# A transformer block's input projection turned from direct products into Strassen's seven block products over two halves of the tokens

## The chip, the cores and the metric

The kernel runs on one core of a Trainium2 chip. The metric is the device time of one execution in microseconds (us); the time of the kernel before is a median over three runs. One more execution was recorded by the hardware profiler, and all rows below are from that one. Matrix products run on TensorE (PE in the rows; PEld is its weight load), element-wise work on VectorE (DVE), ScalarE (ACT) and GpSimd (POOL), and transfers are issued by SyncE (SP) and POOL, in the order of each engine's queue.

## The reference

One block on x of 2048 tokens × 1024 features: RMSNorm, an input projection to 3080 columns, two attentions side by side, an output projection and a SwiGLU FFN. What the change touches is the norm and the projection; the rest consumes its parts.

```python
h = rmsnorm(x, norm1_g[l])
proj = jnp.einsum('bsd,de->bse', h, w_in[l])
dq, dk, dv, fq, fk, fv, fg = jnp.split(proj, SPLITS, axis=-1)
dq = rope_partial(dq.reshape(B, S, DIFF_HEADS, 2, DIFF_DH), cos, sin)
dk = rope_partial(dk.reshape(B, S, DIFF_HEADS, 2, DIFF_DH), cos, sin)
...
log_f = jax.nn.log_sigmoid((fg + b_f[l]).astype(f32))
cum = jnp.cumsum(log_f, axis=1).transpose(0, 2, 1)
```

The parts dq, dk, dv, fq, fk, fv are 512 columns each, fg (the gates) 8. `cum` is a bias of the second attention.

## The kernel before

Every product is made of fp32r operands in pairs: a value is split into a high part (a cast, on ACT) and a low part (the difference, on DVE), and one product becomes three matmuls, high × high, low × high and high × low, that add up in the same PSUM bank (`mm3`, L255 to L257). A matmul has a contraction of 128 and up to 512 columns.

The projection is the first stage (`c1`, L145 to L449). Tokens are in four chunks of 512 (c), each of four rows of 128 (t); features are in eight blocks of the contraction (k). Per chunk, x is loaded (`load_x`), normed (`norm`, `norm_two`: squares on ACT or DVE, the reciprocal root on POOL, a scaling), transposed by PE and evicted straight into the pair `hTh[c]`, `hTl[c]` (`turn`, `turn_two`), which stay in SBUF for the whole stage. Then come, in program order:

- e = 0 to 3 of `w_e` (fq), chunk by chunk, with the norm and the transposes of the next chunk between them;
- e = 4 to 7 (fk); then fv and the gates per row t, from `t_major` with 256 and 264 columns (the last 8 are the gates);
- the gates' log-sigmoid, 16 small transposes and a running sum along tokens (`forget_sums`);
- e = 8 and 9, which hold the rotary features of dq and dk together, with the rope on DVE and POOL;
- e = 10 to 15 (the rest of dq and dk), and dv per row.

`e_major` is 24 matmuls of 512 columns: weights of one e (128 columns of output, which land on the partitions), one chunk of tokens. Each result is split again into a pair (`split_psum`, L141 and L142) and stored to DRAM by POOL, from where the attention stage loads it.

The FFN of the same kernel (`c4`), which the change does not touch, already uses seven block products: a unit there is 7 products of 12 matmuls, in `ORDER` P1, P2, P6, P5, P7, P3, P4, with three PSUM banks (A, B, C) that are added to and taken in between. Its lines L1061 to L1063 are the three matmuls, L1071 and L1073 copies and sums of a bank into `u`, L818 and L819 the splits; L1179 to L1181 are the matmuls of the down projection. Queues of engines are in the order that a list scheduler gives them from program order, data and buffers.

## Time and profile before

| | us |
|---|---|
| median of 3 runs | 2855.63 (2855.2 to 2855.87) |
| the profiled execution | 2852.41 |
| its span | 2850.6 |
| TensorE busy | 2786.9 (98%) |
| VectorE busy | 1706.1 (60%) |
| ScalarE busy | 1359.1 (48%) |
| first product of the projection starts | 10.30 |
| first attention score starts | 571.51 |

The span is the profiled execution from its first to its last instruction on the core, and the execution's own time is 1.8 us longer. The busy time of TensorE is modelled from pipelined matmuls, so 98% does not say that it works at its peak; the distance between starts of matmuls says how fast it goes.

### The profile page before, as it was taken

To read this page: it belongs to the slowest core of one execution; us is meant where nothing else is said; L and a number is where in the kernel's file an instruction comes from. 1 tells how busy PE (TensorE), PEld (TensorE's weight loads), DVE (VectorE), ACT (ScalarE), POOL (GpSimd) and SP (SyncE) were. 2 spreads that over 40 slices of the span, in tenths; PEclk is the share of its full clock that TensorE was granted. 3 is DMA by queue.
4 is the path that set the end of the run, shared out by engine and by line. 5 is a ranking of instruction groups with operands and counts; after the bars stand their busy time and mean duration, and the time that the engine had idled before them with its cause. 6 is when DMAs were issued, how large, how long until landed. Compare 5 with 4: busy or idle time off the path is not lost.

```text
span 2850.6 us, 40932 instructions
## 1 busy us (share of the span) xinstructions
PE 2786.9 (98%) x14538; PEld 2331.8 (82%) x14538; DVE 1706.1 (60%) x3509; ACT 1359.1 (48%) x2764; POOL 613.0 (22%) x1087
## 2 busy tenths in 40 slices
PE   8999999999999999998999999999999999999998
PEld 7889888889989987787877777877888788888887
DVE  5321411088898898887253766665776666665555
ACT  5221211177888787887344333333554433333444
POOL 3210542033434333332111111111000111110001
PEclk9999999999999999999999999999999999999999
DMA  5342444345424332433465544435766333334665
GB/s 195 129 144 90 130 131 126 129 123 145 113 71 123 83 98 77 110 86 118 181 202 196 185 162 160 156 130 194 244 235 223 119 101 103 111 110 133 228 198 173
DMA packets 160860, 410.94 MB, mean 144 GB/s; under 512 B 24544, under 2 KB 41072, under 8 KB 160656
## 3 DMA queue, kind: packets, MB, share of 16 engines
q1 hardware_dynamic: 117488, 282.87, 32.1%
q0 software_dynamic: 43136, 125.45, 12.5%
q8 instruction: 114, 1.87, 0.3%
q14 instruction: 90, 0.74, 0.1%
q10 hardware_dynamic: 32, 0.01, 0.0%
HBM read 274.44 MB, written 133.76 MB: 143 GB/s over the span
## 4 chain that ended last, share of the span: by engine, by line
PE 75%; issue 13%; POOL 4%; ACT 3%; DMA 2%; DVE 2%; POOLq 0%; SPq 0%; DVEq 0%; ACTq 0%
PE psM L257 6%; PE psM L256 6%; PE psM L255 6%; PE ps L709 6%; PE psF L1061 6%; PE psF L1062 5%; PE psF L1063 5%; PE psF L1180 4%; PE psF L1181 4%; PE psF L1179 4%; PE psS L552 4%; PE psS L553 4%; PE psO L644 3%; PE psO L638 2%; PE psO L637 2%
## 5 line engine op out<-in xcount | busy, mean ns | idle before, releaser
L1061 PE MATMUL psF<-hhP,wop 128*128 128x512 f32 x1232 | 478.4, 394 | 16.7 <-DVE u L1073 11.7
L1062 PE MATMUL psF<-hlP,wop 128*128 128x512 f32 x1232 | 480.9, 390 | 0.0
L1063 PE MATMUL psF<-hhP,wop 128*128 128x512 f32 x1232 | 479.9, 390 | 0.0
L582 ACT ACTIVATE p_sb<-p_sb,mx 128x1024 f32<-128x1024 f32 (+7 forms) x384 | 343.7, 901 | 25.0 <-DVE mx L563 17.6
L1061 PEld LDWEIGHTS psF<-hhP,wop 128*128 128x128 f32 x1232 | 231.6, 188 | 83.1 <-DVE u L1073 22.9
L552 PE MATMUL psS<-ks,q 128*128 128x512 f32 (+2 forms) x640 | 271.4, 424 | 3.8 <-DVE mx L569 3.4
L1063 PEld LDWEIGHTS psF<-hhP,wop 128*128 128x128 f32 x1232 | 231.7, 188 | 49.1 <-DVE wop L819 0.2
L1062 PEld LDWEIGHTS psF<-hlP,wop 128*128 128x128 f32 x1232 | 231.8, 188 | 44.8
L709 PE MATMUL ps<-ident,p_sb 128*128 128x128 f32 x1632 | 250.6, 274 | 9.2 <-ACT thd L735 5.3
L1180 PE MATMUL psF<-dop 128*128 128x512 f32 x616 | 239.8, 389 | 0.0
L1181 PE MATMUL psF<-dop 128*128 128x512 f32 x616 | 239.7, 389 | 0.0
L1179 PE MATMUL psF<-dop 128*128 128x512 f32 x616 | 239.7, 389 | 0.0
L553 PE MATMUL psS<-ks,q 128*128 128x512 f32 (+2 forms) x640 | 232.9, 365 | 0.0
L709 PEld LDWEIGHTS ps<-ident,p_sb 128*128 128x128 f32 x1632 | 194.2, 141 | 40.4 <-ACT thd L735 7.5
L255 PE MATMUL psM<-hTh,whi 128*128 128x512 f32 (+1 forms) x528 | 206.1, 392 | 0.4 <-ACT hTh L222 0.3
L256 PE MATMUL psM<-hTl,whi 128*128 128x512 f32 (+1 forms) x528 | 205.6, 390 | 0.6 <-DVE hTl L223 0.5
L257 PE MATMUL psM<-hTh,wlo 128*128 128x512 f32 (+1 forms) x528 | 205.3, 389 | 0.0
L818 ACT CAST wop<-sP 128x512 fp32r<-128x512 f32 x176 | 109.1, 622 | 196.0 <-PE psF L1063 188.3
L818 ACT CAST dop<-wr 128x512 fp32r<-128x512 f32 x154 | 95.5, 620 | 200.0 <-PE psF L1181 185.2
L819 DVE TENSOR_TENSOR dop<-wr,dop 128x512 fp32r<-128x512 f32 x154 | 106.2, 690 | 133.6 <-ACT dop L818 133.4
L1071 ACT COPY u<-psF 128x512 f32<-128x512 f32 x132 | 77.6, 588 | 196.5 <-PE psF L1063 196.5
L819 DVE TENSOR_TENSOR wop<-sP,wop 128x512 fp32r<-128x512 f32 x176 | 120.9, 688 | 81.1 <-ACT wop L818 80.7
(215 smaller groups left out, 6067.4 us busy)
## 6 DMA issues: line engine op xcount, KB each, us to landing
ar<-a_d SPq DMA_DIRECT2D x70, 512.0 KB, 3.5
wr<-in_w_gate_dram SPq DMA_DIRECT2D x44, 512.0 KB, 4.7
wr<-in_w_up_dram SPq DMA_DIRECT2D x44, 512.0 KB, 4.9
a_d<-u POOLq DMA_DIRECT2D x88, 256.0 KB, 3.5
wr<-wd_d SPq DMA_DIRECT2D x40, 512.0 KB, 4.0
a_d<-t POOLq DMA_DIRECT2D x66, 256.0 KB, 2.9
q<-fq_d SPq DMA_DIRECT2D x64, 256.0 KB, 4.1
q<-dq_d SPq DMA_DIRECT2D x64, 256.0 KB, 3.8
```

What stands on the lines that cost most here:

```text
L255: nc.tensor.matmul(ps, lh, rh, start=k == 0, stop=False)
L256: nc.tensor.matmul(ps, lh, rl, start=False, stop=False)
L257: nc.tensor.matmul(ps, ll, rh, start=False, stop=k == DK - 1)
L552: nc.tensor.matmul(pm[:, 0:mw], q[:, m, 0, qc], ks[:, m, cols], start=True, stop=False)
L553: nc.tensor.matmul(pm[:, 0:mw], q[:, m, 1, qc], ks[:, m, cols], start=False, stop=not last)
L709: nc.tensor.transpose(ps[:, (2 * i + s) * P:(2 * i + s + 1) * P], p_of(u, s, m, k0 + i), ident)
L1061: nc.tensor.matmul(acc, o[:, 0, ks_], hh[:, k, :], start=first and k == 0, stop=False, **go)
L1062: nc.tensor.matmul(acc, o[:, 0, ks_], hl[:, k, :], start=False, stop=False, **go)
L1063: nc.tensor.matmul(acc, o[:, 1, ks_], hh[:, k, :], start=False, stop=k == 3, **go)
L1179: nc.tensor.matmul(acc, a[:, 0, bs], w[:, 0, :], start=first and m == 0, stop=False, **go)
L1180: nc.tensor.matmul(acc, a[:, 0, bs], w[:, 1, :], start=False, stop=False, **go)
L1181: nc.tensor.matmul(acc, a[:, 1, bs], w[:, 0, :], start=False, stop=m == NF // 2 - 1, **go)
```

## The change

The projection's stage is written anew. Tokens are in two halves of two chunks, features of the contraction in two halves of four blocks (`kh`), weights in pairs of e; one unit, `Features(half, e)`, makes e and e + 1 for both chunks of a half by seven products of 12 matmuls in place of 96 in `e_major`. `Values(half)` does the same for fv and dv together, with 4 × 12 matmuls for each of the seven products. h is kept only as the seven combined operand pairs (`ops_p`, tiles `phP1`, `plP1` and so on), for one half at a time.

Chunks 0 and 1 with e = 0 to 3 are still made by `e_major`, now from the operands P1, P2 (chunk 0) and P4, P3 (chunk 1). Transposed blocks go to a tile `hb` first (`turn`), from there to DRAM (`hop_d`) and into a split. `quarter` loads blocks of both chunks from `hop_d` as `hr`, makes four differences on DVE, and splits them into P5, P7 and P6, or stores them to DRAM (`tp_d`): P4 of the first half, all four of the second. `load_op` and `put_op` bring them back.

Then 14 units and two halves of values follow: six units of the first half, the values of both halves, eight units of the second half. From the fourth step on, the norm, transposes and quarters of the second half and the sums of value weights (`value_sums`, to `wv_d` in DRAM) run as a generator beside the six first units. The second half's operands take the place of the first half's while the first half's values are made. The gates are 32 matmuls per half with 16 or 8 rows of output and 512 tokens along the columns, so their sum runs along the free side and needs no transposes. The rope's subtract and add move from POOL to DVE.

```diff
+        hop, opp, rawp, hx = pool("hopP", 1), pool("opP", 6), pool("rawP", 4), pool("hx", 6)
...
-        def turn(c, rows, k):
-            ps = psT.tile([P, 512], F32, name="psT")
-            for t4 in range(4):
...
+        def turn(c, q, kh, rows, p=None):
+            b = hxt([P, 4, 256], "hb")
...
                         nc.tensor.transpose(ps[:, (2 * ki + i) * P:(2 * ki + i + 1) * P],
-                                            rows[i][:, (k0 + ki) * P:(k0 + ki + 1) * P], ident)
+                                            rows[i][:, k * P:(k + 1) * P], ident)
...
-                    nc.scalar.activation(hTh[c][:, k, hs], pv, AF.Copy, scale=gcol[:, 0, k:k + 1])
-                    nc.vector.scalar_tensor_tensor(
-                        hTl[c][:, k, hs], pv, gcol[:, 0, k:k + 1], f32(hTh[c][:, k, hs]), ALU.mult, ALU.subtract)
+                    if ki:
+                        nc.vector.tensor_scalar(b[:, k0 + ki, :], pv, gcol[:, 0, k:k + 1], None, ALU.mult)
+                    else:
+                        nc.scalar.activation(b[:, k0 + ki, :], pv, AF.Copy, scale=gcol[:, 0, k:k + 1])
+            nc.gpsimd.dma_start(out=hop_d[c, kh, q], in_=b)
+            if p:
+                cs = slice(q * 256, (q + 1) * 256)
+                split(ops_p[p][0][:, :, cs], ops_p[p][1][:, :, cs], b)
...
+        def quarter(half, q, k0, early):
+            cs, ks_ = slice(q * 256, (q + 1) * 256), slice(k0, k0 + 2)
+            def put(p, src):
+                if early and p != "P4":
+                    hi, lo = ops_p[p]
+                    split(hi[:, ks_, cs], lo[:, ks_, cs], src)
+                else:
+                    nc.gpsimd.dma_start(out=tp_d[p][half, k0 // 2, q], in_=src)
+            b = {}
...
+                    nc.sync.dma_start(out=r[:, kh], in_=hop_d[half * 2 + c, kh, q][:, ks_])
+                    b[kh, c] = r[:, kh]
+            b11, b21, b12, b22 = b[0, 0], b[1, 0], b[0, 1], b[1, 1]
+            yield
+            nc.vector.tensor_sub(b11, b12, b11)
+            nc.vector.tensor_sub(b12, b22, b12)
+            put("P5", b11)
+            put("P7", b12)
+            yield
+            nc.vector.tensor_sub(b22, b22, b11)
+            nc.vector.tensor_sub(b21, b21, b22)
+            put("P6", b22)
+            put("P4", b21)
+            yield
...
+        def load_op(half, p):
+            r = [hxt([P, 4, 256], "hr") for _ in range(2)]
+            for q in range(2):
+                if p in tp_d:
+                    for k in range(2):
+                        nc.sync.dma_start(out=r[q][:, 2 * k:2 * k + 2], in_=tp_d[p][half, k, q])
+                else:
+                    c, kh = dict(P1=(0, 0), P2=(0, 1), P3=(1, 1))[p]
+                    nc.sync.dma_start(out=r[q], in_=hop_d[2 * half + c, kh, q])
+            return p, r
...
+            def multiply(self, p):
+                o, (hh, hl) = self.op.pop(p), ops_p[p]
+                first = p in FIRST_OF
+                if first:
+                    self.bank[FIRST_OF[p]] = bank()
+                acc = self.bank[BANK_OF[p]]
+                for k in range(4):
+                    ks_ = slice(k * P, (k + 1) * P)
+                    go = dict(skip_group_check=not first)
+                    nc.tensor.matmul(acc, o[:, 0, ks_], hh[:, k, :], start=first and k == 0, stop=False, **go)
+                    nc.tensor.matmul(acc, o[:, 0, ks_], hl[:, k, :], start=False, stop=False, **go)
+                    nc.tensor.matmul(acc, o[:, 1, ks_], hh[:, k, :], start=False, stop=k == 3, **go)
...
+            def take(self, p):
+                acc, d = self.bank[BANK_OF[p]], self.dst
+                if p in ("P1", "P6", "P7"):
+                    i = dict(P1=(0, 0), P6=(0, 1), P7=(1, 1))[p]
+                    d[i] = ut()
+                    nc.scalar.copy(d[i], acc)
+                    if p == "P7":
+                        nc.vector.tensor_add(d[1, 1], self.bank["B"], d[1, 1])
+                        self.done(1, 1)
+                elif p == "P2":
+                    nc.vector.tensor_add(d[0, 0], acc, d[0, 0])
+                    self.done(0, 0)
...
+            def multiply(self, p, k):
+                o, (hh, hl) = self.op.pop((p, k)), ops_p[p]
+                first, last = p in FIRST_OF, k == 3
+                if first and k == 0:
+                    self.bank[FIRST_OF[p]] = [bank() for _ in range(4)]
+                for b in range(4):
+                    acc, bs = self.bank[BANK_OF[p]][b], slice(b * P, (b + 1) * P)
+                    go = dict(skip_group_check=not first)
+                    nc.tensor.matmul(acc, hh[:, k, bs], o[:, 0, :], start=first and k == 0, stop=False, **go)
+                    nc.tensor.matmul(acc, hh[:, k, bs], o[:, 1, :], start=False, stop=False, **go)
+                    nc.tensor.matmul(acc, hl[:, k, bs], o[:, 0, :], start=False, stop=last, **go)
...
+        def value_sums(k):
+            r = [raw("wv") for _ in range(2)]
+            for kh in range(2):
+                rows = slice((kh * 4 + k) * P, (kh * 4 + k + 1) * P)
+                for i in range(2):
+                    nc.sync.dma_start(out=r[kh][:, i], in_=w_t[rows, i * 520:i * 520 + 512])
+            yield
+            a11, a12, a21, a22 = r[0][:, 0], r[1][:, 0], r[0][:, 1], r[1][:, 1]
+            o = hlt([P, 2, 512], F32, "vs")
+            nc.vector.tensor_add(o[:, 0], a21, a22)
+            nc.vector.tensor_sub(o[:, 1], o[:, 0], a11)
...
-        turn_two(0, 0, rows[0:2])
+        we = {0: split_e(r0)}
+        for kh in range(2):
+            turn(0, 0, kh, rows[0:2], ("P1", "P2")[kh])
...
-        for c in range(NCH):
-            nxt = [load_x(4 * c + 4 + i) for i in range(4)] if c + 1 < NCH else None
-            for e in range(4):
-                if c == 0 and e < 2:
-                    ps = e_major(we[e], 0, pq[e], halves_[1])
-                else:
-                    ps = e_major(we[e], c)
-                if nxt and e < 2:
...
+        for e in range(4):
+            if e < 2:
+                ps = e_major(we[e], 0, pq[e], halves_[1])
+            else:
+                ps = e_major(we[e], 0)
+            if e < 2:
+                we[e + 2] = split_e((r2, r3)[e])
+                norm_two(nxt[2 * e:2 * e + 2])
+            else:
+                for kh in range(2):
+                    turn(1, e - 2, kh, nxt[2 * (e - 2):2 * (e - 1)], ("P4", "P3")[kh])
+                we[e - 2] = split_e(raw_e(e - 2))
+            give(e, 0, ps)
+        rest = [raw_e(2), raw_e(3)]
+        first = [Features(0, e) for e in (4, 6, 10, 12, 14, 8)]
+        last = [Features(1, e) for e in range(0, 16, 2)]
+        vals = [Values(0), Values(1)]
+        steps = [("in", u, p) for u in first for p in ORDER]
+        n_first = len(steps)
+        for v in vals:
+            steps += [("val", v, p, k) for p in ORDER for k in range(4)]
...
+        for e in range(4):
+            ps = e_major(we[e], 1)
+            if e < 2:
+                we[e + 2] = split_e(rest[e])
+            quarters = quarter(0, e % 2, e // 2 * 2, True)
+            for _ in quarters:
+                pass
+            give(e, 1, ps)
+            if e == 2:
+                advance_loads(0)
+                advance_sums(6)
...
+            z = hxt([P, 2, 512], "gz")
+            for j in range(2):
+                todo_ = [((0, "P1"), (4, "P2")), ((8, "P3"), (12, "P7"))][j]
+                ps = bank()
+                for m, (w0, p) in enumerate(todo_):
+                    hh, hl = ops_p[p]
+                    for k in range(4):
+                        w = gop[:, w0 + k]
+                        st, sp_ = m + k == 0, m == 1 and k == 3
+                        both = w.rearrange("p a b -> p (a b)")
+                        if not sp_:
+                            nc.tensor.matmul(ps[0:16, :], both, hh[:, k, :], start=st, stop=False)
+                        nc.tensor.matmul(ps[0:8, :], w[:, 0, :], hl[:, k, :], start=False, stop=False)
+                        if sp_:
+                            nc.tensor.matmul(ps[0:16, :], both, hh[:, k, :], start=False, stop=True)
+                g, g2 = ut("g"), ut("g2")
+                nc.scalar.copy(g[0:16, :], ps[0:16, :])
+                nc.sync.dma_start(out=g2[0:8, :], in_=g[8:16, :])
...
+            nxt = load(0)
+            yield
+            ahead = []
+            for n, (c, q) in enumerate(todo_):
+                rows, nxt = nxt, None
+                for r in rows:
+                    norm(r)
+                    yield
+                for kh in range(2):
+                    turn(c, q, kh, rows)
+                    yield
+                if n + 1 < len(todo_):
+                    nxt = load(n + 1)
+                for a in ahead:
+                    yield from a
+                ahead = []
+                if c == 3:
+                    ahead = [quarter(1, q, k0, False) for k0 in (0, 2)]
+            for a in ahead:
+                yield from a
+            for k in range(4):
+                yield from value_sums(k)
...
+        for at, s in enumerate(steps):
+            val = s[0] == "val"
+            advance_loads(at)
+            advance_sums(at + 7)
+            advance_splits(at + (3 if val else 4))
+            s[1].multiply(*s[2:])
+            if not val:
+                s[1].take(s[2])
+                if at < n_first:
+                    if at == 0:
+                        waiting.append(load_op(0, "P4"))
+                    elif at == 2:
+                        put_op(*waiting.pop(0))
+                    elif at > 2:
+                        next(bg, None)
+                    if at == n_first - 1:
+                        for _ in bg:
+                            pass
+                        gates(0)
             else:
-                wt = load_t(520, 512)
-            for c in range(NCH):
...
-            nc.scalar.copy(o.rearrange("p h d -> p (h d)"), ps)
-            nc.gpsimd.dma_start(out=dv_d[t * P:(t + 1) * P], in_=o)
```

Three places of the queues, in the kernel's own names. First ScalarE at the very start, before (`xt` is x, `s2` the sums of squares, `whi` the first weights' high part, `hTh0` chunk 0):

```order
L191 ACT_TABLE_LOAD
L191 ACTIVATE psM_153,s2_152<-xt_132 128x512
L191 ACTIVATE psM_163,s2_162<-xt_134 128x512
L199 ACTIVATE xt_132<-xt_132,rstd_151 128x512
L199 ACTIVATE xt_134<-xt_134,rstd_161 128x512
L235 CAST whi_174<-wraw_136 128x1024
L222 ACTIVATE hTh0_121<-psT_178,gcol_80 128x256
L222 ACTIVATE hTh0_121<-psT_187,gcol_80 128x256
```

ScalarE at the same place now (`we` are the first weights, `wop` their pair):

```order
L159 ACT_TABLE_LOAD
L159 CAST wop_195<-we_157 128x512
L222 ACTIVATE psF_174,s2_173<-xt_153 128x512
L222 ACTIVATE psF_184,s2_183<-xt_155 128x512
L229 ACTIVATE xt_153<-xt_153,rstd_172 128x512
L229 ACTIVATE xt_155<-xt_155,rstd_182 128x512
L159 CAST wop_198<-we_157 128x512
L222 ACTIVATE psF_240,s2_239<-xt_159 128x512
L248 ACTIVATE hb_201<-psF_202,gcol_80 128x256
L248 ACTIVATE hb_201<-psF_209,gcol_80 128x256
L248 ACTIVATE hb_219<-psF_220,gcol_80 128x256
```

The cast of half of the first weights moved ahead of the squares, and the transposed blocks go to `hb` first.

Second, VectorE before, behind the last two chunks' norm and around the end of the fourth chunk's query products:

```order
L181 TENSOR_SCALAR xt<-xt,rstd 128x1024
L142 TENSOR_TENSOR hl<-psM,hl 128x512 x2
L207 SCALAR_TENSOR_TENSOR hTl_128<-psT,gcol,hTh_127 128x512 x4
L142 TENSOR_TENSOR hl<-psM,hl 128x512
L207 SCALAR_TENSOR_TENSOR hTl_128<-psT,gcol,hTh_127 128x512 x2
L236 TENSOR_TENSOR wlo<-wraw,whi 128x1024
L207 SCALAR_TENSOR_TENSOR hTl_128<-psT,gcol,hTh_127 128x512 x2
L142 TENSOR_TENSOR hl<-psM,hl 128x512 x4
L338 TENSOR_SCALAR sublnb<-sublnb 128x128
```

VectorE now, at the end of chunk 1's query products (`hr` are loaded blocks, `plP5` to `plP7` low parts of operands, `wop_873` the low part of the first unit's first weights):

```order
L160 TENSOR_TENSOR hl_781<-psF_739,hl_781 128x512
L160 TENSOR_TENSOR plP6_141<-hr_767,phP6_140 128x2x256
L274 TENSOR_TENSOR hr_830<-hr_830 128x512
L160 TENSOR_TENSOR plP5_143<-hr_827,phP5_142 128x2x256
L278 TENSOR_TENSOR hr_830<-hr_830,hr_827 128x512
L160 TENSOR_TENSOR plP7_145<-hr_830,phP7_144 128x2x256
L279 TENSOR_TENSOR hr_827<-hr_827,hr_830 128x512
L160 TENSOR_TENSOR plP6_141<-hr_830,phP6_140 128x2x256
L160 TENSOR_TENSOR hl_844<-psF_802,hl_844 128x512
L637 TENSOR_SCALAR sublnb_81<-sublnb_81 128x128
L646 TENSOR_TENSOR lp_858<-lamv_853 128x128
L160 TENSOR_TENSOR wop_873<-we_786,wop_873 128x512
```

Eviction splits, which stood with norms and transposes, now stand between differences and splits of the quarters, and behind these the first unit's weights.

Third, TensorE before, where a block of transposes of the next chunk stands in the query products:

```order
L257 MATMUL psM<-hTh_121,wlo 128x512
L205 MATMUL psT<-ident,xt 128x128 x8
L255 MATMUL psM<-hTh_121,whi 128x512
L256 MATMUL psM<-hTl_122,whi 128x512
L257 MATMUL psM<-hTh_121,wlo 128x512
```

TensorE now, in the first unit between its products P7 (`phP_144`) and P3 (`phP_146`); `phP_949` is P4:

```order
L431 MATMUL psF<-phP_144,wop 128x512
L240 MATMUL psF<-ident,xt 128x128 x6
L429 MATMUL psF<-phP_949,wop 128x512
L430 MATMUL psF<-plP_950,wop 128x512
L431 MATMUL psF<-phP_949,wop 128x512
L429 MATMUL psF<-phP_949,wop 128x512
L430 MATMUL psF<-plP_950,wop 128x512
L429 MATMUL psF<-phP_146,wop 128x512
```

Transposes that stood between two e now stand inside a unit, and a part of P4 was moved ahead of P3.

## Rows read from the trace of the kernel before

**Rows 1.** The profiled page: busy time by engine, TensorE's granted clock by slices.
```profile
PE 2786.9 (98%) x14538; PEld 2331.8 (82%) x14538; DVE 1706.1 (60%) x3509; ACT 1359.1 (48%) x2764; POOL 613.0 (22%) x1087
...
PEclk9999999999999999999999999999999999999999
```

**Rows 2.** Groups of TensorE, 0 to 572 us: count, busy us, mean ns, idle.
```profile
L255 PE MATMUL psM<-hTh,whi 128*128 128x512 f32 x496 | 196.5, 396 | 0.0
...
L255 PE MATMUL psM<-wt,hTh 128*128 128x512 f32 x128 | 50.5, 394 | 0.0
...
L255 PE MATMUL psM<-wt,hTh 128*128 128x264 f32 x128 | 36.6, 286 | 0.0
```

**Rows 3.** Windows: length, then busy us (count) of each engine, clock, DMA share, GB/s.
```profile
122.00:571.00 449.00, 448.26 (x2318) 381.30 (x2317) 91.50 (x157) 72.58 (x129) 116.85 (x197) 1.00 0.39 124
1557.00:1992.00 435.00, 422.60 (x1841) 342.04 (x1842) 285.99 (x444) 163.09 (x279) 65.53 (x121) 1.00 0.50 167
```

**Rows 4.** Timeline of ScalarE, 71 to 73 us: start, us, instruction, idle before.
```profile
72.19 0.59 ACT L141 CAST hl<-psM 128x512 fp32r<-128x512 f32 x1 [3.23 <-PE psM L257]
```

**Rows 5.** Timeline of ScalarE, 118 to 135 us.
```profile
127.40 0.59 ACT L141 CAST hl<-psM 128x512 fp32r<-128x512 f32 x1 [4.01 <-PE psM L257]
132.95 0.59 ACT L141 CAST hl<-psM 128x512 fp32r<-128x512 f32 x1 [4.96 <-PE psM L257]
```

**Rows 6.** Timeline of TensorE around the first attention score.
```profile
571.51 0.28 PE L552 MATMUL psS<-ks,q 128*128 128x256 f32 x1
```

**Rows 7.** Timeline of all engines from the start.
```profile
4.39 0.60 ACT L191 ACTIVATE psM<-xt 128x512 f32<-128x512 f32 x1 [1.46 <-DMA xt<-in_x_dram]
...
6.85 0.72 ACT L199 ACTIVATE xt<-xt,rstd 128x512 f32<-128x512 f32 x1 [0.42 <-POOL rstd L138]
...
8.68 1.03 ACT L235 CAST whi<-wraw 128x1024 fp32r<-128x1024 f32 x1
...
9.74 1.23 DVE L236 TENSOR_TENSOR wlo<-wraw,whi 128x1024 fp32r<-128x1024 f32 x1 [1.21 <-ACT whi L235]
...
10.30 0.58 PE L255 MATMUL psM<-hTh,whi 128*128 128x256 f32 x1
```

**Rows 8.** Timeline of VectorE in the first FFN half.
```profile
1577.20 0.68 DVE L819 TENSOR_TENSOR wop<-wr,wop 128x512 fp32r<-128x512 f32 x1
1577.80 0.68 DVE L1014 TENSOR_TENSOR sP<-sP,wr 128x512 f32<-128x512 f32 x1
```

**Rows 9.** Timeline of ScalarE in the second FFN half: one unit apart.
```profile
2242.28 0.59 ACT L1071 COPY u<-psF 128x512 f32<-128x512 f32 x1 [2.04 <-PE psF L1063]
...
2261.43 0.59 ACT L1071 COPY u<-psF 128x512 f32<-128x512 f32 x1 [2.04 <-PE psF L1063]
```

**Rows 10.** Timeline of TensorE in the down projection, 69 products apart.
```profile
2029.97 0.39 PE L1179 MATMUL psF<-dop 128*128 128x512 f32 x1
...
2045.61 0.39 PE L1179 MATMUL psF<-dop 128*128 128x512 f32 x1
```

**Rows 11.** Timeline of TensorE: a block of transposes and the next product.
```profile
71.99 1.04 PE L205 MATMUL psT<-ident,xt 128*128 128x128 f32 x8
72.78 0.48 PE L255 MATMUL psM<-hTh,whi 128*128 128x512 f32 x1
```

**Rows 12.** Waits of TensorE, 1540 to 1992 us: total us, times, longest.
```profile
PE psF L1061 <- DVE u L1073: 10.5, 9, 1.9
PE psF L1061 <- DVE hlP L819: 2.5, 1, 2.5
```

**Rows 13.** Timeline of TensorE: attention's first product with values.
```profile
586.00 0.36 PE L637 MATMUL psO<-th,v 128*128 128x256 f32 x1
```

**Rows 14.** DMA issues: queue, count, KB each, median us to landing.
```profile
xt<-in_x_dram SPq DMA_DIRECT2D x16, 512.0 KB, 5.7
...
v<-fv_d SPq DMA_DIRECT2D x8, 1024.0 KB, 5.4
...
h_d<-h2b POOLq DMA_DIRECT2D x14, 512.0 KB, 4.6
```

454 lines of the change are left out of this document (271 added, 183 removed).

## The prediction

> **What bounds the kernel now.** I read the page first: busy times of the engines and the granted clock [rows 1]. TensorE is busy for 2786.9 of 2850.6 us and its clock stands at 9 tenths or more in every slice, so the program ends when TensorE has gone through its queue; VectorE (60%) and ScalarE (48%) matter only where TensorE stands and waits for them. Next the groups of TensorE up to 572 us, shapes apart [rows 2]: three lines of 496 products 512 columns wide, three of 128 such with `wt`, and six groups of 128 that are 256 or 264 wide. Then the windows [rows 3]: from 122 to 571 us TensorE is busy for 448.26 of 449.00 us, so this stretch has no gap to win; it gets shorter by fewer or quicker products alone.
>
> Three places date the stage. The eviction behind the eighth query product (chunk 1, e = 3) starts at 72.19 [rows 4]; two evictions in the middle stand 5.55 us apart for 24 products, 0.2313 us each [rows 5]; the first attention score, right behind the last product, starts at 571.51 [rows 6]. From 72.2 to 571.5 the old program therefore needs 499.3 us. The profiled execution took 2852.41 us, the median of the runs is 2855.63, so I work on the profiled time and add 3.2 at the end.
>
> **What the change does to the queue of TensorE.** In columns over 512: before 1488 + 384 products, 768 of about half that width (390 together) and 96 halves (48) make 2310. After: 8 × 24 classical ones for the first four feature groups, 14 units × 84 (seven block products of 12), values 2 × 336, gates 2 × 32: 2104. So 206 go.
>
> **Up to the first unit.** The order shows the classical products of chunks 0 and 1 with e = 0 to 3 unchanged in number, but their start is later. Before, the first square on ScalarE runs at 4.39, the scaling at 6.85, the weight cast at 8.68, its low half on VectorE from 9.74, and the first product at 10.30 [rows 7]. Now a cast of the first weights stands ahead of the squares; its weights are the third transfer of SP's queue, which was issued 0.9 us behind x. I take 2.5 us for that. Each transposed block now goes through one more step (eviction to `hb`, a 1.03 us cast, a 1.23 us subtract in place of the direct one): 3.2 us more. First product about 16.0, 5.7 later. Before, 61.9 us lay between first product and eighth eviction for 44.4 us of full products and 6 of transposes, so about 11 were lost there; a later start should win back about 4 of them. The eighth product then ends at 73.9. VectorE has about 62 operations up to the last split of chunk 1, then 37 rows of quarters, splits and sums ahead of the low half of the first unit's weights; with one operation of 512 elements every 0.60 us [rows 8] these are about 60 us from 4.4 on, so they end at about 64 if they never wait, at 74 with 10 us of waiting. I take **F = 74** for the first unit, between 68 (all 11 us won back but one) and 82 (the quarters, which go to DRAM and return, end 8 us later).
>
> **From F on.** A unit of the later FFN has the same form: 84 products in 19.15 us, 0.228 each [rows 9]. 14 units: 268.2. Values have the form of the down projection, 69 products from 2029.97 to 2045.61, 0.2267 each [rows 10]: 672 of them are 152.3. The 64 gate products have 16 or 8 rows of output but still 512 columns, at the same price 14.5. The later half's 64 transposes stay on the queue: 8 take 0.79 us [rows 11], so 6.3. Together 441.3.
>
> **Which rate.** The 0.2313 of the old products and the 0.2267 to 0.228 of the FFN are different forms in the same trace; the new products are written as the FFN's, but the stage is the old one's, with other transfers. If they ran at 0.2313, 1912 products would cost 7.7 more. I take half, +4, bounds 0 and 8. The Trainium skill, "TensorE: Matmul & The Clock Gate", section "Wait — 56ns, not 53.3ns?", says that warm matmuls start N ÷ 2.4 GHz plus about 2.5 ns apart, 215.7 ns at 512 columns, for any form. This trace does not agree in size: [rows 5] have 231.3 and [rows 10] 226.7. By that rule only the 206 products count, 44.4 us instead of 58 less 4, an estimate which would put the result near 2830; the measured rows decide.
>
> **Stalls.** The first half of the FFN's feature stage, with the background work beside it, takes 435 us for 422.60 busy [rows 3]: 12.4 us over 22 units, of which 10.5 are nine or so waits of product P3 for P7's taking on VectorE and 2.5 one operand split [rows 12]. Here six units have background work, and the same P7–P3 gap: in the first of them the order puts six transposes and five products of P4 behind P7, 0.6 + 1.1 = 1.7 us of cover, where no transposes are left only the products. VectorE: 18 operations a unit, 108, plus 16 evictions, 16 quarter differences, 16 sums of value weights and 12 rope operations, 168 × 0.60 = 101 us of the 115 us of six units; in the FFN's half it is 286 of 435. So more waits than there: I take **16 us**, lower bound 4 (eight units at the later rate without waits), upper bound 29 (1.9 us, the longest such wait, at each of 14 units' gaps, and one split of 2.5).
>
> The rope's subtract and add go from POOL to VectorE and are in the 12; POOL's freed time buys nothing. The splits of the later half's operands are put between the first half's value products. VectorE has there 28 weight splits, 12 sums and 8 splits of results, 48 × 0.60, and 12 splits of 1024 at 1.23 or less [rows 7], 44 of 76 us: hidden; without that cover one such split is 1.2 us of TensorE's time.
>
> **Handover.** Keys, queries and values of attention lie over the operand tiles, which come free only in the last unit. The values are needed 14.5 us after attention's first score [rows 6, 13] and their load takes 5.4 [rows 14], so they fit; +1, bounds 0 and 5.
>
> **Sum.** 74 + 441.3 + 4 + 16 = 535.3, against 571.5: 36.2 less, 35.2 with the handover. 2852.4 − 35.2 = 2817.2, and with the 3.2 to the median **2820 us**. The four uncertain terms together (6, 4, 12, 1 down; 8, 4, 13, 4 up, by squares) give 2806 to 2837 for this case.
>
> **Rivals.**
> 1. *VectorE becomes the bound in the first six units.* It takes work in order, and waits for casts, transfers and accumulators: in the FFN's half it idles (435 − 286) / 22 = 6.8 us per unit [rows 3]. If these waits come on top of 101 / 6 = 16.9 us, a unit takes 23.7 instead of 19.15, 27 us over six, some 8 of them already among the stalls: 2839. For it speaks the added background; against it that VectorE's waits in the FFN are mostly slack that it can close.
> 2. *The chain x → norm → transpose leads (slower).* TensorE's transposes stand in its own queue; behind them wait products that need nothing of x. One pair costs a load of 5.7 us [rows 14], four squares of 0.60, 1.9 from the end of a square to the scaling, and two scalings of 1024, priced as the cast of 1.03 [rows 7]: 12.1. If each pair starts only when the last one is turned, 48 us are added, less what is hidden: with none hidden 2868. It decides from 10.2 us per pair, where 35.2 + 5.7 is eaten. Against it: if the six buffers go round, the second pair's x lies in those of P4's operand and can be loaded before the first pair is turned; the third pair waits for the stores of the first one's turned blocks, 4.6 us [rows 14] and an eviction of 0.5, and with the 12.1 it needs 17 us, while between the first pair's last transpose and the third's first the order has 85 products and 16 transposes, 21 us.
> 3. *No rate gain.* The products run at the old 0.2313: +3.7, 2824, inside the first case's range.
> 4. *Fewer stalls.* Transposes cover the P7–P3 gap fully and F is early: 2797 to 2806.
>
> **Numbers.** Forecast with rival 3: 0.75; rival 1 (2837 to 2850): 0.13; rival 4: 0.06; rival 2 and beyond: 0.06, of it 0.05 slower and 0.01 within. A measurement of this kernel can tell about 0.2% (5.7 us) from no change. Rival 1 in its worst tail gives another 0.01 within. Faster 0.93, same 0.02, slower 0.05. The range 2803 to 2842 leaves out about half each of rivals 4 and 1, and rival 2.
>
> **What would show it.** The first product of the stage near 16 us and the first unit near 74; ScalarE's evictions of one unit 19.2 us apart in the later half; value products 0.227 apart; the first score near 536; TensorE waiting in the first six units for VectorE, up to 2 us at a time, 8 to 20 us in all. Wrong would be: waits of transposes for scaled x of over 3 us, VectorE above 95% in the first six units, a first unit after 82, or products at 0.231.

## The result and the profile after

The changed kernel takes 2875.58 us (median of 4 runs, 2871.93 to 2882.39) against 2855.41 beside it: ratio 1.0079, 95% interval 1.0055 to 1.0103. It is slower by 20 us where 35 less were forecast. All profile numbers below are of its profiled execution of 2875.7 us, span 2873.9.

The page of the changed kernel, as [rows 1] of before: busy times, busy tenths of TensorE in 40 slices of 72 us, and the granted clock.

```profile
PE 2757.9 (96%) x13938; PEld 2284.1 (79%) x13938; DVE 1915.9 (67%) x3818; ACT 1501.2 (52%) x3004; POOL 635.9 (22%) x1141
...
PE   7788999999999999998999999999999999999997
...
PEclk9999999999999999999999999999999999999999
```

TensorE is busy for 29 us less than before, and yet the span is 23.3 longer: it stands, in the first four slices above all. When the stage begins (timeline of TensorE), when its value products run (in the row, the pair behind the three durations: first and last start) and when attention's first score starts, beside [rows 7] and [rows 6]:

```profile
10.15 1.11 PE L240 MATMUL psF<-ident,xt 128*128 128x128 f32 x4 [5.04 <-ACT xt L229]
...
16.62 0.58 PE L327 MATMUL psF<-phP,wop 128*128 128x256 f32 x1 [2.11 <-ACT phP L159]
```

```profile
L488 PE MATMUL psF<-wop,phP x224: 387/389/632, 254.9 to 416.9; 128*128 128x512 f32 x112
```

```profile
582.82 0.35 PE L865 MATMUL psS<-ks,q 128*128 128x256 f32 x1 [0.28 <-DMA q<-fq_d]
```

The stage ends at 582.8, not at 571.5 as before or 535.3 as forecast. The windows of its parts: six units of the first half, their end with the first gates, value products, second gates, eight units of the later half. Columns as in [rows 3].

```profile
77.00:231.00 154.00, 127.94 (x546) 102.31 (x546) 92.64 (x156) 72.60 (x142) 60.47 (x110) 0.91 0.75 246
231.00:255.00 24.00, 16.20 (x59) 9.20 (x58) 15.51 (x26) 5.70 (x10) 6.78 (x13) 0.79 0.72 250
255.00:417.00 162.00, 155.87 (x671) 127.56 (x670) 93.25 (x133) 77.52 (x122) 30.32 (x54) 0.98 0.66 232
417.00:431.00 14.00, 14.00 (x63) 8.38 (x62) 7.55 (x12) 5.50 (x9) 1.76 (x4) 1.00 0.49 152
431.00:583.00 152.00, 148.63 (x648) 119.92 (x647) 95.66 (x145) 64.22 (x108) 53.67 (x92) 1.00 0.54 166
```

The first two windows hold the loss. Their pure work is 115 (units) + 6.3 (transposes) + 7.25 (gates) = 128.5 us; from the first unit's start at 77.3 to the first value product at 254.9 there are 177.6, so 49 are lost. TensorE was busy for 127.94 + 16.20 = 144.1 of them, 15.6 more than the work needs: the granted clock was 0.91 and 0.79 on average there, that is, TensorE ran for part of the time at the lower of its two levels (1.2 GHz), behind each of the longer waits. The other 34 us are waits. Waits of TensorE in 77 to 255 us, as [rows 12]:

```profile
PE psF L429 <- ACT u L439: 10.9, 2, 7.2
PE psF L240 <- ACT xt L213: 10.6, 5, 4.9
PE psF L431 <- DVE wop L160: 6.4, 1, 6.4
PE psF L429 <- DVE u L441: 5.2, 2, 4.1
```

The longest of them shows how such a wait comes about. VectorE, ScalarE and TensorE around 207 us:

```profile
203.47 0.69 DVE L274 TENSOR_TENSOR hr<-hr 128x512 f32<-128x512 f32 x1 [8.01 <-DMA tp_dP<-hr]
```

```profile
206.04 0.62 ACT L159 CAST hl<-u 128x512 fp32r<-128x512 f32 x1 [10.81 <-DVE u L444]
206.57 0.58 ACT L439 COPY u<-psF 128x512 f32<-128x512 f32 x1
```

```profile
207.20 0.80 PE L429 MATMUL psF<-phP,wop 128*128 128x512 f32 x1 [7.24 <-ACT u L439]
207.79 0.63 PE L430 MATMUL psF<-plP,wop 128*128 128x512 f32 x1
208.22 0.63 PE L431 MATMUL psF<-phP,wop 128*128 128x512 f32 x1
```

VectorE stands 8.01 us in front of a difference of a quarter, until a transfer of the quarters has landed (a store, by the row); behind it stands the sum that ScalarE's next split needs, so ScalarE stands 10.81 us; behind that split stands the copy of product P6 out of its bank, and TensorE, which is to add P7 to that bank, waits 7.24 us for the copy. Nothing that TensorE does here needs the quarter. Behind the wait its matmuls start 0.43 us apart (207.79, 208.22) in place of 0.227, at a granted clock of 0.57 from 204 to 212 us.

Past the stage three things differ. From the first score to the FFN's first product there are 993.6 us (582.8 to 1576.4), 985.7 before (571.5 to 1557.2). The FFN up to the last down product takes the same (1282.2 and 1282.5). Behind the last recorded work 4.3 us are added. 11.3 + 7.9 − 0.3 + 4.3 make the 23.3 us of the span but for rounding.

### The profile page after: what moved, and what is told of

Its sections match the earlier page's. It is cut to its first block, busy times and chain, and to the rows that moved or that the text cites. A ratio compares the mean times of both kernels' runs of the same rounds, so it can differ in the third digit from the quotient of the medians.

```text
span 2873.9 us, 40778 instructions
## 1 busy us (share of the span) xinstructions
PE 2757.9 (96%) x13938; PEld 2284.1 (79%) x13938; DVE 1915.9 (67%) x3818; ACT 1501.2 (52%) x3004; POOL 635.9 (22%) x1141
## 4 chain that ended last, share of the span: by engine, by line
PE 67%; issue 14%; DMA 4%; POOL 4%; ACT 3%; DVE 2%; SPq 0%; POOLq 0%; DVEq 0%; ACTq 0%
PE ps L1022 6%; PE psF L1359 6%; PE psF L1360 5%; PE psF L1361 5%; PE psF L1479 4%; PE psF L1478 4%; PE psF L1477 4%; PE psS L865 4%; PE psS L866 4%; PE psO L957 3%; PE psO L951 2%; PE psO L950 2%; ACT p_sb L895 2%; PE psF L429 2%; PE psF L430 2%
## 5 line engine op out<-in xcount | busy, mean ns | idle before, releaser
L159 ACT CAST wop<-sP 128x512 fp32r<-128x512 f32 x232 | 143.9, 621 | 235.8 <-PE psF L1361 188.8
L160 DVE TENSOR_TENSOR wop<-sP,wop 128x512 fp32r<-128x512 f32 x232 | 159.2, 687 | 101.5 <-ACT wop L159 101.0
L429 PE MATMUL psF<-phP,wop 128*128 128x512 f32 x392 | 158.0, 407 | 19.9 <-ACT u L439 12.7
L142 DVE TENSOR_TENSOR th<-ps,th 128x512 fp32r<-128x512 f32 (+1 forms) x232 | 146.9, 650 | 32.5 <-ACT th L141 31.6
L1401 POOL DMA_DIRECT2D a_d<-u x88 | 47.6, 541 | 532.1 <-DVE u L1392 529.4
```

The lines of the kernel that those rows point to most:

```text
L159: nc.scalar.copy(hi, src)
L160: nc.vector.tensor_sub(lo, src, f32(hi))
```

## The experiments

Theory A: the later half's preparation, put beside the first six units, holds TensorE through the in-order queues of ScalarE, VectorE and POOL, and the clock falls behind the waits. Rival B: the six units wait by themselves. Later two views of A were set against each other: D (the transfers beside it make its way through DRAM slow) and E (the order of waits in the queues). The first value product and the first score date the stage in each run's profile; "ratio" is to the kernel before, run beside it on the same chip, whose median was 2855.4 beside the changed kernel and 2850.9 to 2853.5 beside the others.

| run | median us | ratio, 95% interval | first value product | first score |
|---|---|---|---|---|
| changed kernel | 2875.6 | 1.0079, 1.0055 to 1.0103 | 254.9 | 582.8 |
| e1_no_prep | 2829.2 | 0.9913, 0.9896 to 0.9929 | 221.5 | 540.4 |
| e2_no_quarters | 2864.9 | 1.0044, 1.0029 to 1.0060 | 258.8 | 580.5 |
| e4_rstd_on_dve | 2860.2 | 1.0029, 1.0018 to 1.0040 | 245.3 | 574.5 |
| e6_no_value_sums | 2851.3 | 0.9995, 0.9986 to 1.0005 | 244.4 | 566.2 |
| e3_later_loads | 2872.5 | 1.0069, 1.0049 to 1.0089 | 253.1 | 584.3 |
| e5_sums_spread | 2853.4 | 0.9994, 0.9982 to 1.0005 | 244.9 | 568.2 |
| e7_sums_in_values | 2874.7 | 1.0074, 1.0058 to 1.0089 | 248.3 | 590.1 |
| e8_light_units_first | 2871.0 | 1.0062, 1.0045 to 1.0079 | 249.5 | 578.8 |
| e9_loads_ahead | 2862.6 | 1.0035, 1.0022 to 1.0048 | 261.9 | 582.0 |
| e10_and_first_unit | 2862.5 | 1.0037, 1.0025 to 1.0050 | 256.1 | 576.5 |
| e11_first_unit_only | 2874.4 | 1.0079, 1.0063 to 1.0094 | 257.9 | 586.4 |
| e12_no_first_stores | 2887.6 | 1.0123, 1.0106 to 1.0140 | 242.7 | 582.9 |
| e13_one_store | 2885.9 | 1.0119, 1.0105 to 1.0133 | 240.6 | 579.9 |
| e14_spread_light_later | 2851.1 | 0.9997, 0.9986 to 1.0007 | 247.1 | 568.7 |
| e15_spread_and_rstd | 2840.9 | 0.9959, 0.9946 to 0.9973 | 234.5 | 558.2 |
| e16_root_on_dve | 2848.9 | 0.9990, 0.9981 to 0.9999 | 243.2 | 563.2 |
| e17_and_light_later | 2850.2 | 0.9996, 0.9985 to 1.0006 | 244.2 | 565.7 |

Profiles of one execution differ in parts that no edit touches: the FFN up to its last down product took from 1275 to 1283 us in them. So a difference of medians under 5 us says little here, and the two dates are the surer sign for the stage.

**e1_no_prep.** In the background generator the loop over the four pairs is empty, and the loads and splits of the later half's operands are gone:

```diff
-            for n, (c, q) in enumerate(todo_):
+            for n, (c, q) in enumerate(()):
```

> Left out: the later half's x loads, norm, transposes, quarters and operand splits; its units run on the first half's operands. The value sums stay. Theory A (the later half's preparation, run beside the first six units through the in-order queues of ScalarE, VectorE and POOL and through DRAM, makes TensorE wait and its clock fall): the first value product, at 254.9 us in the changed kernel, comes near 210, and the time falls from 2875.6 to 2825 to 2835. Rival B (the six units wait by themselves, for their own banks, sums and weights): the first value product stays after 240 and the time above 2858.

2829.2 us, first value product at 221.5:

```profile
L488 PE MATMUL psF<-wop,phP x224: 387/389/403, 221.5 to 373.2; 128*128 128x512 f32 x112
```

By the time A holds, and B's range is missed: the preparation costs 46 us in all, 33 of them up to the first value product and 10 among the value products, where its splits stood (221.5 to 373.2 is 151.7 us, against 162.0 from 254.9 to 416.9). But B is not empty. From the first unit (76.0) to the first value product there are still 145.5 us for 122.2 of work (115 and 7.25, no transposes), so 23 of the 49 us of loss stay, 15 of them waits and the rest a lower clock, nearly all of it before 200 us:

```profile
77.00:200.00 123.00, 107.68 (x440) 85.86 (x440) 81.77 (x132) 47.59 (x83) 42.55 (x74) 0.92 0.68 218
```

So of the 33 us some 26 are lost time that went, 6.3 the work of the transposes left out, and 1.3 an earlier first unit. The waits that stay are 6.4 us in the first unit and 1.9 and 5.7 around 123 and 140 us, where this run has the value sums (POOL stores them from 103 to 132 us). What the units cost by themselves and what the sums cost them was not told apart here.

**e2_no_quarters.** One line of the generator, and the operand loads and splits as in e1:

```diff
-                    ahead = [quarter(1, q, k0, False) for k0 in (0, 2)]
+                    pass
```

> Left out: only the later half's quarters (loads from DRAM, four differences, stores) and operand splits; x, norm, transposes and the stores of the turned blocks stay, and the later half runs on the first half's operands. Theory A1 (within A, the quarters' way through DRAM is the larger part: VectorE stood 8.0 us for a quarter, ScalarE 10.8 behind it, TensorE 7.2): 2835 to 2850. A2 (the chain x, norm, transposes is the larger part: 16 us of TensorE's waits carry its name): 2855 to 2868.

A2's figure, 2864.9, but not its reason alone: the first value product is not earlier (258.8), and the gain lies among the value products (258.8 to 411.0, 152 us). So A1 falls. The wait at 207 us that I had traced to a quarter was one turn that the chain took, not its length: without the quarters the time before the first value product is spent in other waits (8.5 us at 204 us and 9.5 at 235, both for ScalarE's copies). The value sums still stand at the end in this run.

**e4_rstd_on_dve.**

```diff
-            nc.gpsimd.tensor_tensor(ss, s2[:, 0:1], s2[:, 1:2], ALU.add)
-            rstd_of(r, ss, 1)
+            nc.vector.tensor_tensor(ss, s2[:, 0:1], s2[:, 1:2], ALU.add)
+            nc.vector.tensor_scalar(r, ss, 1.0 / D, EPS, ALU.mult, ALU.add)
```

> The three small operations of the norm that stand in POOL's queue (sum, mean with epsilon, root) become two on VectorE; the reciprocal root itself is left out. Everything else stays. If the scaled x is late because POOL's queue holds these operations behind stores that wait for their splits (waits of 4.9 and 3.8 us of transposes), those waits fall below 1 us and the time to 2860 to 2868; if x lands late or VectorE is no quicker, they stay and the time is 2870 to 2882.

2860.2, and the transposes' waits for the later half's scaled x fall from 10.6 us to this:

```profile
PE psF L240 <- ACT xt L213: 2.3, 2, 1.3
```

The longest is now 1.3 us, where under 1 was expected. The norm's small operations had stood in POOL's queue behind stores. For the last pair of the changed kernel the squares were done at 169.5 us, and POOL came to their sums at 174.73, behind 15 issues of stores in a row:

```profile
165.85 4.77 POOL L341 DMA_DIRECT2D dq_d<-hl  x8 [1.28 <-ACT hl L159]
170.62 1.69 POOL L263 DMA_DIRECT2D tp_dP<-hr  x3
172.30 2.42 POOL L341 DMA_DIRECT2D dq_d<-hl  x4
174.73 0.35 POOL L211 TENSOR_TENSOR ss<-s 128x1 f32<-128x1 f32 x2
```

The run also leaves out the root itself, so it does not tell POOL's queue from POOL's time for the root (0.7 us a row); e16 below keeps the root.

**e6_no_value_sums** (all seven value products take plain weights) and **e5_sums_spread**, which leaves nothing out and moves the four sums:

```diff
                 for kh in range(2):
                     turn(c, q, kh, rows)
                     yield
+                yield from value_sums(n)
...
-            for k in range(4):
-                yield from value_sums(k)
```

> Left out: the sums of value weights (loads, 16 operations on VectorE, stores); the value products take the plain weights from the input. If the end of the first half is held by these sums and their place in the four weight buffers (ScalarE stood 7.8 and 5.4 us for value weights before TensorE's waits of 3.7 and 4.1 at 236 and 242 us), the first value product comes 12 to 20 us earlier and the time is 2853 to 2865; if the units are late for other reasons, under 5 us change.

> Nothing left out. The four value sums stand one behind each pair's transposes, in place of all four at the end of the six units. If their cost (24 us by the run without them) was that they stood together at the end, in the buffers and queues that the first value weights need, the first value product comes 8 to 15 us earlier and the time is 2855 to 2867. If it is their work and transfers as such, the waits move into the middle units and the time stays within 5 us of 2875.

2851.3 and 2853.4: the sums as such cost almost nothing, their place at the end costs 22 us. Both beat their ranges, and both have the first value product 10 us earlier (12 to 20 were expected of e6). The value products of e5 take 155.2 us in place of 162.0, with the later half's operand splits still among them:

```profile
L488 PE MATMUL psF<-wop,phP x224: 387/389/499, 244.9 to 400.1; 128*128 128x512 f32 x112
```

**e3_later_loads, e8_light_units_first, e7_sums_in_values.** Three other orders: the constants 10 and 7 of weight loads and sums to 8 and 5; the units as e = 4, 6, 14, 12, 10, 8; the value sums in the first three steps of the value products.

```diff
-                if loads[0] >= at + (10 if s[0] == "in" else 6):
+                if loads[0] >= at + (8 if s[0] == "in" else 6):
...
-            advance_sums(at + 7)
+            advance_sums(at + 5)
```

```diff
-        first = [Features(0, e) for e in (4, 6, 10, 12, 14, 8)]
+        first = [Features(0, e) for e in (4, 6, 14, 12, 10, 8)]
```

```diff
+        vs = (y for k in range(4) for y in value_sums(k))
...
+                if at - n_first < 3:
+                    for _ in range(4):
+                        next(vs, None)
```

> Nothing left out. Weights of a unit are loaded 8 steps ahead in place of 10, and their sums made 5 steps ahead in place of 7, so SyncE's queue reaches a weight load later, when its buffer is nearer to free. SyncE stood 76 us in front of weight loads that waited for VectorE's splits, with x loads behind them. If that holds the x chain, x lands earlier and the time falls to 2858 to 2870; if the chain hangs on POOL and the stores, it stays within 2870 to 2882, or rises as the sums wait for the later loads.

> Nothing left out. The order of the first half's units becomes e = 4, 6, 14, 12, 10, 8: the units with eight stores per result (e = 10 and 12) come behind the x chain. If the norm's small operations are late because POOL issues those stores ahead of them, the wait of 3.8 us for the fourth pair falls below 1 and the time to 2866 to 2872; if the stores hold the quarters' stores instead, later, it stays at 2872 to 2882.

> Nothing left out. The value sums move behind the six units, into the first three steps of the value products, whose first two products (22 us) use plain weights. By the crowding theory the six units end 8 to 12 us earlier, VectorE has slack among the value products, and the time is 2853 to 2866. By the rival the sums' way through DRAM is then late for the third product P6, TensorE waits there 5 to 15 us, and the time is 2870 to 2885.

2872.5 and 2871.0, each under 5 us below the changed kernel. e3 did not do what it was to do: SyncE's waits in front of the units' weight loads were 76.4 us from 16 to 255 us and are 73.4 with the edit, so what they cost is not shown. In e8 the waits for the fourth pair fall from 3.8 us to 1.9 (two of them), and the first value product comes 5 us earlier. In e7 (2874.7) the sums then hold the value products, which take 175 us (248.3 to 423.0), as its rival said.

**e9_loads_ahead** (x of the next pair ahead of the value sums, both quarters' loads ahead of their work, and the two rows of a pair normed in one step of the generator in place of two), **e11_first_unit_only** (splits of the first unit's first two weights ahead of the last quarter, the first weights' cast behind the scaling) and **e10_and_first_unit** (both):

```diff
             if e == 2:
                 advance_loads(0)
                 advance_sums(6)
+                advance_splits(2)
...
+            tc.keep_in_program_order(nc.scalar.copy(o[:, 0, :], r0[:, kh]))
```

```diff
                 if n + 1 < len(todo_):
                     nxt = load(n + 1)
+                for a in ahead:
+                    next(a)
+                yield from value_sums(n)
```

> Nothing left out. As e5, and in the background work the next pair's x is loaded ahead of the value sums, and both quarters of a half load their blocks before either is worked on, some steps ahead of use. In e5 VectorE still stood 10 us for a quarter's block and the transposes 6 us for scaled x. If the wait for transfers, not the work, is what holds the queues, the first value product comes 8 to 15 us earlier than in e5 (near 233 us) and the time is 2838 to 2848. If the engines' work or the amount of transfers is the limit, the waits move and the time stays within 4 us of e5's 2853.

> Nothing left out. The two edits at the start alone, on the changed kernel. The same 4 to 8 us against 2875 if the start's loss is passed on to the end; 0 to 2 us if the waits of the background chain take it up.

> Nothing left out. As e9, with two edits at the start: the first weights' cast stands behind the scaling of x, and the low halves of the first unit's first two weights are made ahead of the last quarter of chunk 1. TensorE's wait of 6.4 us in the first unit should shrink below 2 and the first product come about 2 us earlier, so 4 to 8 us less than e9. If VectorE's backlog only moves to the third product of the unit, 0 to 3 us less.

Neither gained. e9 is 9 us slower than e5: the first value product came at 261.9, behind waits of TensorE of 11.2 us at 187 us, for a copy on ScalarE, and of 7.0 at 229, for a sum on VectorE, which had stood 5.4 us for a quarter's load. What brought the first of them was not followed. In e11 the wait of 6.4 us of the first unit is gone and the first product comes at 15.3, yet the first value product is no earlier, since the other waits grow to

```profile
PE psF L429 <- ACT u L439: 17.3, 5, 7.2
PE psF L240 <- ACT xt L213: 13.9, 7, 4.9
```

The growth lies mostly in the first 30 us: 4.1 us at 88 us and 2.4 at 103. From 112 to 212 us the two traces stand within 0.7 us of each other, with the same waits (4.9 us at 142, 3.8 at 178, 7.2 at 207). That is the clearest sign of what leads: up to 255 us it is the background chain that sets the pace, and TensorE's time won ahead of it is waited away.

**e12_no_first_stores** and **e13_one_store.** In `give` and `turned` (for e12; e13 has one store of the whole tile in place of `pass`):

```diff
+            elif c < 2:
+                pass
+            else:
+                for cc in (c - 2, c):
```

> The results of the first half's six units are not stored; the later half's units store theirs twice, in both places. So the first six units have none of the stores of results, 12 MB and their issues on POOL, and the later half has them twice. Theory D (the background chain is slow because its stores and loads queue behind other transfers and issues: from 77 to 255 us a store of a turned block takes 6.3 us to land and a load of a quarter 6.0, while 247 GB/s are moved): the first value product comes near 225, from 254.9. Rival E (the chain is slow by the order of waits on ScalarE, VectorE and POOL, whatever else is moved): it stays after 245. The whole time may hold less, since the later half has more to store.

> As e12, but each result of the first half's units is stored once, with the same bytes in one transfer of long rows to a place of its own. If D holds through POOL's issues and short rows, the first value product is near that of e12; if through the bytes, it is near 245 to 255.

Transfers in 77 to 255 us of the changed kernel (packets; then KB and median us to landing), of e12 and of e13:

```profile
DMA packets 17593, 43.89 MB, mean 247 GB/s; under 512 B 4020, under 2 KB 4020, under 8 KB 17582
...
hp_d<-hb POOLq DMA_DIRECT2D x8, 512.0 KB, 6.3
hr<-hp_d SPq DMA_DIRECT2D x16, 256.0 KB, 6.0
```

```profile
DMA packets 13262, 35.27 MB, mean 198 GB/s; under 512 B 1696, under 2 KB 1696, under 8 KB 13252
...
hp_d<-hb POOLq DMA_DIRECT2D x8, 512.0 KB, 4.7
hr<-hp_d SPq DMA_DIRECT2D x16, 256.0 KB, 3.4
```

```profile
DMA packets 16864, 48.37 MB, mean 272 GB/s; under 512 B 2068, under 2 KB 2068, under 8 KB 16853
...
hp_d<-hb POOLq DMA_DIRECT2D x8, 512.0 KB, 5.0
hr<-hp_d SPq DMA_DIRECT2D x16, 256.0 KB, 3.7
```

Between D and E: the first value product comes 12 and 14 us earlier, not 30. e13 moves more bytes than the changed kernel (48.37 against 43.89 MB) with fewer short packets, and its blocks land as fast as in e12, 3.7 us against 6.0. So the bytes are not what slowed them; the many stores are, by their number (POOL's issues) or by their short rows. These two come together here and were not told apart; that the loads `hr`, which SyncE issues, land sooner speaks for the short rows. The Trainium skill, "DMA: Bandwidth & Descriptors", section "Latency and other measured facts", says that the latency of an HBM access is 0.2 us on average and 2 us at high load. As an explanation of the 6.0 us this does not fit e13, where the load is higher and the landing quicker. The whole time of both is longer, since the later half stores everything twice: in e12 its units and gates take 177 us in place of 166, and right behind the first score TensorE stands 21.5 us for a split of VectorE. So the first score does not date the end of the stage in these two.

**e14, e15, e16, e17.** e14 is e5 with e3 and e8; e15 is e5 with e4; e16 is e5 with the whole norm of the later half on VectorE (the core below); e17 is e14 with the same.

```diff
-            rstd_of(r, ss, 1)
+            nc.vector.tensor_scalar(ss, ss, 1.0 / D, EPS, ALU.mult, ALU.add)
...
+            nc.vector.tensor_scalar(sh.bitcast(i32), ss.bitcast(i32), 1, None, ALU.logical_shift_right)
+            nc.vector.tensor_scalar(r.bitcast(i32), sh.bitcast(i32), -1.0, float(0x5f3759df), ALU.mult, ALU.add)
+            for _ in range(3):
+                nc.vector.scalar_tensor_tensor(tt, r, ss, r, ALU.mult, ALU.mult)
+                nc.vector.tensor_scalar(tt, tt, -0.5, 1.5, ALU.mult, ALU.add)
+                nc.vector.tensor_tensor(r, r, tt, ALU.mult)
```

> Nothing left out. e5 (value sums spread) with the two edits that alone gave 3 and 5 us: weights of a unit loaded 8 steps ahead with sums 5 ahead, and the units with eight stores per result last. If the gains add, 2844 to 2849, below the kernel before by 0.2 to 0.3%; if the later loads hurt where the sums now stand, 2852 to 2862.

> e5 (value sums spread) with the norm's small operations on VectorE and without the reciprocal root, which is left out. If the two parts are separate costs, their gains add: 2875 less 22 less 15, 2836 to 2842. If they are two views of one chain, the time is 2846 to 2854.

> Nothing left out. e5 (value sums spread) with the later half's norm on VectorE throughout: the reciprocal root comes from a shift, a subtraction and three Newton steps, 14 small operations a row in place of three on POOL. If these cost VectorE little (112 operations of about 0.1 us, some 11 us over the six units, beside the waits that they remove), the time is within 4 us of the run without the root, 2838 to 2845, faster than the kernel before by 0.3 to 0.5%. If they stand in VectorE's way, 2846 to 2856.

> Nothing left out. e16 with the loads and the order of units of e14. If those two edits still give the 2 us that they gave on e5, 1 to 4 us below e16; with the x chain short they may give nothing, or delay the sums: up to 5 us above e16.

The two known parts nearly add: 2840.9 in e15, 35 below the changed kernel, where e5 and e4 alone gave 22 and 15. e14's two edits do not add to e5. With the root computed it is 2848.9: the 13 small operations a row (the expectation counted 14) give back 8 us, more than the 4 that I allowed. They take 0.15 to 0.21 us each, 16.5 us of VectorE in all, where 11 were allowed. First value product of e16:

```profile
L496 PE MATMUL psF<-wop,phP x224: 387/389/501, 243.2 to 397.0; 128*128 128x512 f32 x112
```

e16 is the version that leaves nothing out and is below the kernel before, by 0.1% (0.9990, interval up to 0.9999), which is 3.8 us and so no clear gain. e5, e14 and e17 are level with the kernel before.

## Why the prediction was wrong, step by step

**The queue of TensorE and its rates: right.** The later half's units stand 19.19 us apart (forecast 19.155), shown by ScalarE's copies of one product in two units, as in [rows 9]:

```profile
460.88 0.59 ACT L439 COPY u<-psF 128x512 f32<-128x512 f32 x1 [2.15 <-PE psF L431]
...
480.07 0.59 ACT L439 COPY u<-psF 128x512 f32<-128x512 f32 x1 [2.15 <-PE psF L431]
```

The eight units and second gates take 165.7 us (417.1 to 582.8) against 160.4. The value products start 0.2267 us apart (104 of them from 299.66 to 323.01). So nothing of the +4 for the rate was needed. The 215.7 ns that the prediction quotes from the Trainium skill, "TensorE: Matmul & The Clock Gate", section "Wait — 56ns, not 53.3ns?", do not show: 19.19 / 84 = 228 ns. The page gives its rule by columns alone; "for any form" is the prediction's wording. That fewer products save time shows in e1, which is 24 us under the kernel before, and the 64 transposes that it leaves out account for 6.3 of them at most.

**Up to the first unit: right within its bounds.** First product at 16.62 (forecast 16.0), first unit at 77.3 (74). But 2 us into it TensorE waited 6.4 us for the low half of a weight, behind VectorE's quarters; e11 showed that this cost nothing in the end, as long as the background work leads.

**Stalls: the step that failed.** "I take 16 us, lower bound 4, upper bound 29" was measured at 64 (49 in the six units with their gates, 10 in the value products, 5 in the rest). It was sized from the waits at the P7–P3 gap in the FFN, 1.9 us at most. That gap held TensorE here too, but as one place among several: 1.1 us in the first unit, and in the last one 3.7 for the copy and 4.1 for the sum of P7:

```profile
235.96 0.79 PE L429 MATMUL psF<-phP,wop 128*128 128x512 f32 x1 [3.70 <-ACT u L439]
242.14 0.80 PE L429 MATMUL psF<-phP,wop 128*128 128x512 f32 x1 [4.10 <-DVE u L441]
```

These 8.9 us are a quarter of the 34 us of waits; the others are for scaled x, for a weight and for the copy of P6. What the FFN's first half did not have is a chain of background work that had to be finished by the last unit. The step treated this work as load (101 of 115 us of VectorE); VectorE was busy for only 92.64 of 154 us there. Its cost was the order: each operation waits for a transfer or a store in an in-order queue, and what TensorE needs stands behind it. Of the 64, the place of the value sums accounts for 10 to the first value product and 15 to the first score (e5), the norm on POOL for 8 to 10 (e4, without the root). The 10 us among the value products go with the later half's operand splits left out (e1 and e2, 152 us), but 7 of them also with the sums moved and the splits kept (e5, 155.2), so these are not separate shares. And no term held the clock, 15.6 us in the six units. It is not all accounted for: e15, which has the sums moved and the norm off POOL, still has its first value product at 234.5, 29 us behind 77.0 + 128.5, and what these hang on was not taken apart.

In sum, the stage ends 47.5 us later than forecast: 3.3 for the first unit, 48.3 for the stalls, less the 4 for the rate. The handover below, the end of the program (4.3) and the FFN (−0.3) make it the 58.5 us by which the profiled execution missed its 2817.2.

**The rivals.** Rival 1 had the right engines and six units, and 2839 by waits of 6.8 us a unit; its mechanism, waits of the in-order queues on top of the work, is nearest to what happened, but it was given 0.13, lacked the clock and saw only VectorE. Rival 2 is right in part, and of the prediction's own signs of being wrong it is the one that came: transposes waited 10.6 us in all for scaled x, up to 4.9 for one pair, over the 3 us named, though not 10.2 for each pair. The hidden margin that I counted (21 us for 17) was gone; off POOL these waits fall to 2.3 (e4). That a chain leads (e11) is rival 2's idea too, but its chain ended at the transposes and lacked the quarters and the sums. The result fell into the 0.05 that the prediction gave to slower.

**Handover: +1, bounds 0 to 5, was 7.9.** The values were not late (first product 15.9 us after the first score, 14.5 before, with a wait of 0.2 for their load). The clock fell: the first 40 us of attention before, and after:

```profile
571.00:591.00 20.00, 15.85 (x110) 12.66 (x110) 12.28 (x42) 13.60 (x36) 5.74 (x10) 1.00 0.81 223
591.00:611.00 20.00, 20.00 (x137) 17.01 (x136) 19.52 (x59) 16.10 (x36) 5.10 (x9) 1.00 0.48 146
```

```profile
582.00:602.00 20.00, 14.95 (x86) 11.05 (x85) 12.43 (x43) 13.86 (x35) 5.82 (x10) 0.88 1.06 337
602.00:622.00 20.00, 20.00 (x125) 17.60 (x125) 15.60 (x45) 12.24 (x26) 6.00 (x9) 0.87 1.00 256
```

The transfer engines are at 1.06 and 1.00 of their share (0.81 and 0.48 before): all loads of attention fall together, since their buffers come free in the last unit. And TensorE runs part of these 40 us at the lower clock, 0.50 from 598 to 606 us. Its waits hardly differ (about 5 us in the first 20, 4 before); why the clock fell here and not before, no run shows. The k-th score starts 11.3 us later than before at the first one and 16.3 later at 612 us, so 5.0 us are lost here; the other 3 are spread over attention.

## What to carry to other kernels

Work that is put beside a bound engine is priced by its chain, not by its busy time alone: list, for every operation that the bound engine waits for, what stands ahead of it in its queue and on which transfer that in turn waits. A stall sized from another stage holds only if the background work there has the same deadline. And where TensorE's clock falls behind a wait, the wait costs again: 34 us of waits cost 49 here.

## What the hardware showed unexpectedly

The last recorded operation ends 4.1 us before the span's end in the kernel before and 8.5 us in the changed one:

```profile
2845.71 0.75 DVE L1211 SCALAR_TENSOR_TENSOR x<-x,rstd,normfb 128x512 f32<-128x512 f32 x1 [0.71 <-POOL rstd L138]
```

```profile
2864.68 0.75 DVE L1509 SCALAR_TENSOR_TENSOR x<-x,rstd,normfb 128x512 f32<-128x512 f32 x1 [0.72 <-POOL rstd L138]
```

Spans end at 2850.6 and 2873.9. Nothing that the trace records lies in the added 4.3 us. In the profiles of the other kernels this end is 7.1 to 8.5 us too, and only in e13 3.6; it stays open. More bytes did not slow the blocks' way through DRAM; many stores of short rows beside them went with the slower landing: 6.0 us at 247 GB/s with 4020 packets under 512 B, 3.7 at 272 with 2068.
